# Moving each tile of a log-softmax as two transfers, its even and its odd partitions

## The chip, the cores and the metric

The kernel runs on one core of a Trainium2 chip. The core has five engines that take instructions of their own: PE (TensorE), DVE (VectorE), ACT (ScalarE), POOL (GpSimd) and SP (SyncE), and 16 DMA engines, which move data between the chip's main memory (HBM) and the core's on-chip buffer (SBUF, 128 partitions). The metric is the device time of one execution in microseconds (us). The kernel before takes 7580.06 us, the median of 8 runs between 7571.31 and 7588.07 us. The profile comes from one further execution, recorded by the hardware profiler, which took 7638.0 us.

## What is computed

A log-softmax along the last axis of a tensor of 16 x 512 x 50000 float32 numbers:

```python
def reference(x):
    max_x = np.max(x, axis=-1, keepdims=True)
    shifted = x - max_x
    log_sum_exp = np.log(np.sum(np.exp(shifted), axis=-1, keepdims=True))
    return (shifted - log_sum_exp).astype(np.float32)
```

The input and the output have 8192 rows of 50000 numbers each, 1638.40 MB read and as much written.

## The kernel before

**Tiles.** A tile is 32 rows. Each row is cut into four quarters of 12500 numbers, and a quarter is one partition: partition p holds quarter p mod 4 of row p div 4 (lines 73 and 74). So a tile fills 128 partitions with 12500 numbers (50000 bytes) each, 6.4 MB in all, and lies in main memory without a gap. There are 256 tiles and four buffers (`bufs`, line 93); tile t uses buffer t mod 4, and the result is written over the input in the same buffer.

**Loads.** SP issues them. The first tile comes as two transfers of half the columns each (lines 150 to 154), the next three as one transfer each (line 156). Then a loop (lines 158 to 161) waits for `stored[j]` to reach 16 (the helper `take`, line 47, which also takes the count back) and issues the load of the next tile into buffer j (line 148). A load adds 16 to `landed[j]` when it has landed, one for each DMA engine.

**Work on a tile.** DVE waits for `landed[j]` (line 201, by way of `take`), reduces four column blocks of 3125 numbers to their negated maxima (line 206), and joins these to one maximum for each row with a few small instructions (lines 171 to 186). ACT exponentiates each column block as its maximum is ready, with the sum accumulated beside it (line 248), and then makes four factors that bring the blocks' sums to the common maximum (line 256). DVE multiplies (line 217), PE adds up the four partitions of a row with a matrix of ones and zeros (line 285), ACT takes the logarithm (line 239), and DVE subtracts maximum and logarithm from the whole buffer in place (line 191).

**Stores.** ACT issues them (line 243): it waits until DVE has subtracted, issues one transfer for the buffer, and the transfer adds 16 to `stored[j]` when it is done. The last tile alone is subtracted and stored in four column blocks (lines 219, 278 and 279).

**Order.** There is no planner: each engine has its list of instructions, and semaphores tie the lists together. Loads go through the DMA queue of SP (q1 in the profile), stores through that of ACT (q10), each in the order of its engine's list. ACT has, for each tile, four exponentials, two small instructions and then the store; what is queued behind a store on ACT is the first exponential of the next tile.

Of the kernel before, what the change touches and what calls it, by code (L numbers as in the profile page):

```python
# [19 lines left out]
NBUF = 4  # L20

NS = 4

HEAD = 2

# [19 lines left out]
def take(engine, sem, n=16):  # L45

    engine.wait_ge(sem, n).then_inc(sem, -n)  # L47


def cols(c):  # L50
    return slice(c * C, (c + 1) * C)


@with_exitstack
def kernel(
# [9 lines left out]
    W = V // G  # L65
    assert N % R == 0 and W == NS * C
    ntiles = N // R
# [5 lines left out]
    xt = xf.rearrange("(t r) (g w) -> t (r g) w", r=R, g=G)  # L73
    ot = of.rearrange("(t r) (g w) -> t (r g) w", r=R, g=G)

    def run(a, first, n):

        part = a[first : first + NBUF * n].rearrange("(q i) p w -> q i p w", i=NBUF)
        return lambda q, i: part[bass.ds(q, 1), i].rearrange("o p w -> (o p) w")
# [13 lines left out]
    bufs = [data.tile([P, W], FP32, name=f"buf{j}") for j in range(NBUF)]  # L93
# [4 lines left out]
    def each(n, width, name):  # L98
        return [stats.tile([P, width], FP32, name=f"{name}{j}") for j in range(n)]

    negms, parts, scales, scaleds = (
        each(NBUF, NS, n) for n in ("negm", "part", "scale", "scaled")
    )
# [9 lines left out]
    def sem(name):  # L113
        return ctx.enter_context(nc.semaphore(name))

    landed = [sem(f"landed{j}") for j in range(NBUF)]
    stored = [sem(f"stored{j}") for j in range(NBUF)]
    heads = [sem(f"head{h}") for h in range(HEAD)]
    ready = sem("ones_ready")
    on_dve = Count(sem("on_dve"))  # L120
# [7 lines left out]
    subtracted = Count(sem("subtracted"))  # L128
# [3 lines left out]
    @block.gpsimd  # L132
    def _(gpsimd):
        view = ones.rearrange("p (r g) -> p r g", g=G)
        gpsimd.memset(ones, 1.0).then_inc(ready)  # L135
        gpsimd.affine_select(  # L136
            out=view, in_=view, pattern=[[-G, R], [0, G]], base=0,
            channel_multiplier=1, compare_op=ALU.is_ge, fill=0.0,
        ).wait_op(ready, 1, "sem-ge").then_inc(ready)
        gpsimd.affine_select(  # L140
            out=view, in_=view, pattern=[[G, R], [0, G]], base=G - 1,
            channel_multiplier=-1, compare_op=ALU.is_ge, fill=0.0,
        ).wait_op(ready, 2, "sem-ge").then_inc(ready)

    @block.sync
    def _(sync):
        def load(j, src):
            sync.dma_start(out=bufs[j], in_=src).then_inc(landed[j], 16)

        for h in range(HEAD):  # L150
            part = slice(h * W // HEAD, (h + 1) * W // HEAD)
            sync.dma_start(
                out=bufs[0][:, part], in_=xt[0][:, part]
            ).then_inc(heads[h], 16)
        for t in range(1, NBUF):
            load(t, xt[t])
        src = run(xt, NBUF, rounds)
        with sync.Fori(0, rounds) as q:
            for j in range(NBUF):
                take(sync, stored[j])  # L160
                load(j, src(q, j))
        for j in range(NBUF - 1):
            take(sync, stored[j])
        take(sync, stored[NBUF - 1], 16 * NS)

    @block.vector
    def _(vector):
        def share(k):

            on_dve.next(  # L170
                vector.transpose(out=allneg, in_=negp.to_broadcast([P, SQ]))  # L171
            ).then_inc(on_dve.sem)
            on_dve.next(
                vector.tensor_reduce(  # L174
                    out=rowneg, in_=allneg.rearrange("p (r g) -> p r g", g=G),
                    op=ALU.min, axis=AX,
                )
            ).then_inc(on_dve.sem)
            on_dve.next(
                vector.tensor_copy(  # L180
                    out=spread.rearrange("p (r g) -> p r g", g=G),
                    in_=rowneg[:, :, None].to_broadcast([P, SQ // G, G]),
                )
            ).then_inc(on_dve.sem)
            on_dve.next(
                vector.transpose(out=negmaxs[k], in_=spread)  # L186
            ).then_inc(agreed.sem)

        def subtract(k, *bufs):
            for n, buf in enumerate(bufs):  # L190
                ins = vector.tensor_scalar(  # L191
                    out=buf, in0=buf, scalar1=negmaxs[k][:, 0:1], scalar2=logs[k],
                    op0=ALU.add, op1=ALU.subtract,
                )
                if n == 0:
                    logged.next(ins)
                ins.then_inc(subtracted.sem)

        def whole(j, first=False, by_pieces=False):
            if not first:  # L200
                take(vector, landed[j])

            for c in range(NS):
                if first and c % (NS // HEAD) == 0:
                    take(vector, heads[c // (NS // HEAD)])
                vector.tensor_reduce(  # L206
                    out=negms[j][:, c : c + 1], in_=bufs[j][:, cols(c)],
                    op=ALU.max, axis=AX, negate=True,
                ).then_inc(shifted.sem if c < NS - 1 else on_dve.sem)
            on_dve.next(vector.nop()).then_inc(shifted.sem)  # L210
            vector.tensor_reduce(  # L211
                out=negp, in_=negms[j], op=ALU.min, axis=AX
            ).then_inc(on_dve.sem)
            share(j)

            rescaled.next(
                vector.tensor_mul(out=scaleds[j], in0=scales[j], in1=parts[j])  # L217
            ).then_inc(summed.sem)
            subtract(j, *([bufs[j][:, cols(c)] for c in range(NS)] if by_pieces else [bufs[j]]))

        def settle():
            for count in (on_dve, rescaled, logged):
                count.settle(vector)

        for j in range(NBUF):
            whole(j, first=j == 0)
        settle()
        with vector.Fori(0, rounds - 1):
            for j in range(NBUF):
                whole(j)  # L230
            settle()
        for j in range(NBUF):
            whole(j, by_pieces=j == NBUF - 1)

    @block.scalar
    def _(scalar):
        def log(k):
            added.next(
                scalar.activation(out=logs[k], in_=rowsums[k], func=ACT.Ln)  # L239
            ).then_inc(logged.sem)  # L240

        def store(j, dst, buf):
            subtracted.next(scalar.dma_start(out=dst, in_=buf)).then_inc(stored[j], 16)

        def whole(j):
            for c in range(NS):
                shifted.next(
                    scalar.activation(  # L248
                        out=dump, in_=bufs[j][:, cols(c)], func=ACT.Exp,
                        bias=negms[j][:, c : c + 1], scale=1.0,  # L250
                        accum_out=parts[j][:, c : c + 1],
                    )
                ).then_inc(on_act.sem)
                on_act.next(scalar.nop())  # L254
            agreed.next(
                scalar.activation(  # L256
                    out=scales[j], in_=negms[j], func=ACT.Exp,
                    bias=negmaxs[j][:, 0:1], scale=-1.0,
                )
            ).then_inc(rescaled.sem)  # L260
            log(j)

        def settle():
            for count in (on_act, shifted, agreed, added, subtracted):
                count.settle(scalar)

        nc.scalar.preload_act_table_set("natural_log_exp_and_others")  # L267
        dst = run(ot, 0, rounds)
        with scalar.Fori(0, rounds) as q:
            for j in range(NBUF):  # L270
                whole(j)
                store(j, dst(q, j), bufs[j])
            settle()
        for j in range(NBUF - 1):
            whole(j)
            store(j, ot[ntiles - NBUF + j], bufs[j])
        whole(NBUF - 1)
        for c in range(NS):
            store(NBUF - 1, ot[ntiles - 1][:, cols(c)], bufs[NBUF - 1][:, cols(c)])

    @block.tensor
    def _(tensor):
# [47 lines left out]
```

## Time and profile before

| What | Value |
|---|---|
| Median of 8 runs | 7580.06 us |
| The profiled execution | 7638.0 us, its span 7636.3 us |
| DVE busy | 5441.3 us (71% of the span) |
| ACT busy | 3184.7 us (42%) |
| PE busy | 477.9 us (6%) |
| Moved by DMA | 3276.85 MB, mean 429 GB/s |
| Median from issue to landing | load 44.4 us, store 48.5 us |

The span is the profiled execution from its first to its last instruction. An engine's busy time is the sum of its instructions; waiting is not counted. The page cuts the span into 40 equal slices, and in the row named DMA each digit is the busy share of the 16 DMA engines in a slice, in tenths, where 9 is 90% or more. A "packet" is one piece of a transfer that one DMA engine moves. "SPq" and "ACTq" are the instruction queues of SP and ACT, which wait and issue transfers; in a row such as "A <- B: 973.8, 253, 11.4", A waited for B for 973.8 us in total, 253 times, 11.4 us at the longest.

### The profile page before, as it was taken

What the parts mean: (1) busy time and instruction counts of PE and PEld (TensorE: products, weight loads), DVE (VectorE), ACT (ScalarE), POOL (GpSimd) and SP (SyncE); (2) the same over time, 40 slices, a digit from 0 to 9 for tenths busy, and PEclk for the clock granted to TensorE, in tenths of its full rate; (3) what the DMA queues carried; (4) which work ended last, traced back from release to release, by engine and by line L of the source; (5) the groups of instructions that cost most, each with busy time, mean ns of one, the idle gap of its engine ahead of it and who ended that gap; (6) DMA issues with size and microseconds to landing.
All of it is one profiled execution on the core that took longest, in us unless ns stands there. A gap on an engine that the chain in (4) does not pass through costs nothing. (4 is left out here: it accounts for less than half of the span.)

```text
span 7636.3 us, 14069 instructions
## 1 busy us (share of the span) xinstructions
PE 477.9 (6%) x2048; PEld 456.0 (6%) x2048; DVE 5441.3 (71%) x2819; ACT 3184.7 (42%) x2561; POOL 1.4 (0%) x7
## 2 busy tenths in 40 slices
PE   0000000000000000000000000000000000000000
PEld 0000000000000000000000000000000000000000
DVE  7777777777777777777777777777777777777766
ACT  4344444444344343434444344443434434444333
POOL 0000000000000000000000000000000000000000
DMA  9999999999999999999999999999999999999998
GB/s 427 432 435 433 435 433 435 433 435 433 434 432 432 433 432 435 432 434 433 434 433 429 431 427 430 429 428 431 432 427 431 428 428 430 427 426 427 427 414 368
DMA packets 74306, 3276.85 MB, mean 429 GB/s; under 512 B 8256, under 2 KB 8256, under 8 KB 8256
## 3 DMA queue, kind: packets, MB, share of 16 engines
q1 hardware_dynamic: 37008, 1638.42, 50.3%
q10 hardware_dynamic: 37296, 1638.42, 49.6%
q14 instruction: 2, 0.02, 0.0%
HBM read 1638.40 MB, written 1638.40 MB: 429 GB/s over the span
## 5 line engine op out<-in xcount | busy, mean ns | idle before, releaser
L248 ACT ACTIVATE dump<-buf,negm 128x3125 f32<-128x3125 f32 x1024 | 2937.2, 2868 | 3856.1 <-DVE negm L206 3758.6
L206 DVE TENSOR_REDUCE negm<-buf 128x1 f32<-128x3125 f32 x1024 | 3418.4, 3401 | 973.9 <-DVEq L47 973.8
L191 DVE TENSOR_SCALAR buf<-buf,negmax,logsum 128x12500 f32<-128x12500 f32 (+1 forms) x259 | 1739.0, 6715 | 553.8 <-ACT logsum L239 553.8
L285 PE MATMUL sums<-scaled,ones 128*128 128x1 f32 x2048 | 477.9, 355 | 7138.3 <-DVE scaled L217 7138.3
L285 PEld LDWEIGHTS sums<-scaled,ones 128*128 128x128 f32 x2048 | 456.0, 328 | 7160.1 <-DVE scaled L217 7160.1
L217 DVE TENSOR_TENSOR scaled<-scale,part 128x4 f32<-128x4 f32 x256 | 41.6, 163 | 580.2 <-ACT scale L256 580.2
L239 ACT ACTIVATE logsum<-sums 128x1 f32<-128x1 f32 x256 | 43.8, 171 | 551.1 <-PE sums L285 551.1
L248 ACT ACTIVATION_READ_ACCUMULATOR dump<-buf,negm 128x1 f32 x1024 | 190.8, 186 | 0.0
L256 ACT ACTIVATE scale<-negm,negmax 128x4 f32<-128x4 f32 x256 | 76.1, 297 | 23.6
L211 DVE TENSOR_REDUCE negp<-negm 128x1 f32<-128x4 f32 x256 | 40.2, 157 | 39.2 <-DVE negm L206 39.2
L186 DVE STREAM_TRANSPOSE negmax<-spread 128x32 f32<-128x32 f32 x256 | 54.2, 212 | 8.9
L171 DVE STREAM_TRANSPOSE allneg<-negp 128x32 f32<-128x32 f32 x256 | 54.2, 212 | 8.9
L174 DVE TENSOR_REDUCE rowneg<-allneg 128x8 f32<-128x32 f32 x256 | 47.7, 186 | 8.9
L180 DVE COPY spread<-rowneg 128x32 f32<-128x32 f32 x256 | 46.4, 181 | 8.9
L267 ACT ACT_TABLE_LOAD x1 | 1.3, 1283 | 1.0 <-SPq L111 1.0
L136 POOL TENSOR_SCALAR_AFFINE_SELECT ones<-ones 128x128 f32<-128x128 f32 x1 | 0.5, 519 | 0.1
L140 POOL TENSOR_SCALAR_AFFINE_SELECT ones<-ones 128x128 f32<-128x128 f32 x1 | 0.5, 519 | 0.1
L135 POOL MEMSET ones<- 128x128 f32 x1 | 0.2, 205 | 0.5 <-SPq L111 0.5
L314 POOL MEMSET const-bfloat16-1.0<- 128x1 bf16 x1 | 0.1, 103 | 0.0
L314 POOL MEMSET const-uint8-127<- 128x1 uint8 x1 | 0.1, 103 | 0.0
L314 POOL MEMSET const-float32-0.0<- 128x1 f32 x1 | 0.1, 99 | 0.3 <-issue 0.3
L314 POOL MEMSET const-float32-1.0<- 128x1 f32 x1 | 0.1, 99 | 0.0
## 6 DMA issues: line engine op xcount, KB each, us to landing
buf<-in_x_dram SPq DMA_DIRECT2D x255, 6250.0 KB, 44.4
out_dram<-buf ACTq DMA_DIRECT2D x255, 6250.0 KB, 48.5
buf<-in_x_dram SPq DMA_DIRECT2D x2, 3125.0 KB, 13.7
out_dram<-buf ACTq DMA_DIRECT2D x4, 1562.5 KB, 8.1
```

What stands on the lines that cost most here:

```text
L171: vector.transpose(out=allneg, in_=negp.to_broadcast([P, SQ]))
L174: vector.tensor_reduce(out=rowneg, in_=allneg.rearrange("p (r g) -> p r g", g=G), op=ALU.min, axis=AX,)
L180: vector.tensor_copy(out=spread.rearrange("p (r g) -> p r g", g=G), in_=rowneg[:, :, None].to_broadcast([P, SQ // G, G]),)
L186: vector.transpose(out=negmaxs[k], in_=spread)
L191: ins = vector.tensor_scalar(out=buf, in0=buf, scalar1=negmaxs[k][:, 0:1], scalar2=logs[k], op0=ALU.add, op1=ALU.subtract,)
L206: vector.tensor_reduce(out=negms[j][:, c : c + 1], in_=bufs[j][:, cols(c)], op=ALU.max, axis=AX, negate=True,).then_inc(shifted.sem if c < ...
L211: vector.tensor_reduce(out=negp, in_=negms[j], op=ALU.min, axis=AX).then_inc(on_dve.sem)
L217: vector.tensor_mul(out=scaleds[j], in0=scales[j], in1=parts[j])
L239: scalar.activation(out=logs[k], in_=rowsums[k], func=ACT.Ln)
L248: scalar.activation(out=dump, in_=bufs[j][:, cols(c)], func=ACT.Exp, bias=negms[j][:, c : c + 1], scale=1.0, accum_out=parts[j][:, c : c + 1],
L256: scalar.activation(out=scales[j], in_=negms[j], func=ACT.Exp, bias=negmaxs[j][:, 0:1], scale=-1.0,)
L285: ins = tensor.matmul(rowsums[j], ones, scaleds[j][:, c : c + 1], start=c == 0, stop=c == NS - 1,)
```

## The change

Each load and each store of a whole tile becomes two transfers: one of the 64 even partitions, one of the 64 odd ones. Each buffer has two semaphores for its stores, one for each half, and SP issues the load of a half as soon as the store of that half is done. DVE still waits for the whole tile: both loads add to the same `landed[j]`, and it now waits for 32. The first tile's load and the last tile's store stay as they were.

```diff
+H = 2
+def half(a, h):
+    return a.rearrange("(q h) w -> q h w", h=H)[:, h, :]
...
-    stored = [sem(f"stored{j}") for j in range(NBUF)]
+    stored = [[sem(f"stored{j}_{h}") for h in range(H)] for j in range(NBUF)]
...
-        def load(j, src):
-            sync.dma_start(out=bufs[j], in_=src).then_inc(landed[j], 16)
+        def load(j, src, h):
+            sync.dma_start(
+                out=half(bufs[j], h), in_=half(src, h)
+            ).then_inc(landed[j], 16)
...
         with sync.Fori(0, rounds) as q:
             for j in range(NBUF):
-                take(sync, stored[j])
-                load(j, src(q, j))
+                for h in range(H):
+                    take(sync, stored[j][h])
+                    load(j, src(q, j), h)
...
-                take(vector, landed[j])
+                take(vector, landed[j], 16 * H)
...
         def store(j, dst, buf):
-            subtracted.next(scalar.dma_start(out=dst, in_=buf)).then_inc(stored[j], 16)
+            for h in range(H):
+                ins = scalar.dma_start(out=half(dst, h), in_=half(buf, h))
+                if h == 0:
+                    subtracted.next(ins)
+                ins.then_inc(stored[j][h], 16)
```

More of the change, by code (lines that the diff above doesn't have):

```diff
@@ L155, in _ @@
         for t in range(1, NBUF):
-            load(t, xt[t])
+            for h in range(H):
+                load(t, xt[t], h)
         src = run(xt, NBUF, rounds)
@@ L159, in _ @@
             for j in range(NBUF):
-                take(sync, stored[j])
-                load(j, src(q, j))
+                for h in range(H):
+                    take(sync, stored[j][h])
+                    load(j, src(q, j), h)
         for j in range(NBUF - 1):
-            take(sync, stored[j])
-        take(sync, stored[NBUF - 1], 16 * NS)
+            for h in range(H):
+                take(sync, stored[j][h])
+        take(sync, stored[NBUF - 1][0], 16 * NS)
     @block.vector
@@ L242, in store @@
         def store(j, dst, buf):
-            subtracted.next(scalar.dma_start(out=dst, in_=buf)).then_inc(stored[j], 16)
+            for h in range(H):
+                ins = scalar.dma_start(out=half(dst, h), in_=half(buf, h))
+                if h == 0:
+                    subtracted.next(ins)
+                ins.then_inc(stored[j][h], 16)
         def whole(j):
@@ L278, in _ @@
         for c in range(NS):
-            store(NBUF - 1, ot[ntiles - 1][:, cols(c)], bufs[NBUF - 1][:, cols(c)])
+            subtracted.next(
+                scalar.dma_start(
+                    out=ot[ntiles - 1][:, cols(c)], in_=bufs[NBUF - 1][:, cols(c)]
+                )
+            ).then_inc(stored[NBUF - 1][0], 16)
     @block.tensor
```

## Prediction

> **What bounds the kernel now.** I read the page from the top: busy times, the 40 slices, then the DMA queues.
>
> ```profile
> span 7636.3 us, 14069 instructions
> PE 477.9 (6%) x2048; PEld 456.0 (6%) x2048; DVE 5441.3 (71%) x2819; ACT 3184.7 (42%) x2561; POOL 1.4 (0%) x7
> ...
> DMA  9999999999999999999999999999999999999998
> GB/s 427 432 435 433 435 433 435 433 435 433 434 432 432 433 432 435 432 434 433 434 433 429 431 427 430 429 428 431 432 427 431 428 428 430 427 426 427 427 414 368
> DMA packets 74306, 3276.85 MB, mean 429 GB/s; under 512 B 8256, under 2 KB 8256, under 8 KB 8256
> ...
> q1 hardware_dynamic: 37008, 1638.42, 50.3%
> q10 hardware_dynamic: 37296, 1638.42, 49.6%
> ```
>
> No compute engine is full, and the DMA engines are: the two queues' packets take 50.3% and 49.6% of the 16 engines' time, 99.9% together. The packet counts tell what a packet is. 257 loads on 16 engines make 4112 small packets, one for each engine to raise the semaphore, and 255 x 128 + 2 x 128 = 32896 data packets, one for each partition; the sum is 37008. The stores' 37296 come out likewise (255 x 128 + 4 x 128 + 259 x 16). So a partition's 50000 bytes are one packet. A load packet takes 0.503 x 16 x 7636.3 / 32896 = 1.87 us on average; the trace's packet records give a median of 1.847 us for both directions, and 9 ns for a small packet. 65536 packets' worth of data (50000 bytes each) on 16 engines at 1.847 us make 7565 us. That is 71 us less than the span, and only 15 us less than the median of the runs shown.
>
> Next, is a DMA engine ever without work? I asked for the DMA share by stretches; of each row the last two numbers are the share and the GB/s.
>
> ```profile
> 1000.00:2000.00 1000.00, 63.47 (x272) 60.55 (x272) 716.95 (x374) 422.79 (x340) 0.00 (x0) 1.00 1.00 434
> 5000.00:6000.00 1000.00, 63.49 (x272) 60.57 (x272) 710.14 (x368) 412.96 (x334) 0.00 (x0) 1.00 1.00 430
> 7000.00:7400.00 400.00, 26.14 (x112) 24.94 (x112) 277.75 (x148) 164.51 (x134) 0.00 (x0) 1.00 1.00 423
> 7500.00:7560.00 60.00, 3.74 (x16) 3.57 (x16) 40.90 (x22) 24.87 (x20) 0.00 (x0) 1.00 0.99 406
> 7560.00:7600.00 40.00, 1.86 (x8) 1.78 (x8) 25.58 (x13) 12.43 (x10) 0.00 (x0) 1.00 0.79 329
> 7600.00:7636.00 36.00, 1.87 (x8) 1.78 (x8) 19.11 (x14) 12.44 (x10) 0.00 (x0) 1.00 0.65 275
> ```
>
> The share is 1.00 up to about 7500 us. The slower late stretches are slower packets, mostly loads, not idle engines. Only the last 76 us have idle DMA time: 0.21 x 40 + 0.35 x 36 = 21 us.
>
> Last, the waits, DVE's and SP's, and the time of a transfer from issue to landing.
>
> ```profile
> DVE negm L206 <- DVEq L47: 973.8, 253, 11.4
> ```
> ```profile
> SPq L47 <- SPq L47: 7480.2, 256, 69.2
> ```
> ```profile
> buf<-in_x_dram SPq DMA_DIRECT2D x255, 6250.0 KB, 44.4
> out_dram<-buf ACTq DMA_DIRECT2D x255, 6250.0 KB, 48.5
> ```
>
> DVE waits 3.85 us per tile for the load. SP does nothing but wait for stores. But with about 29.6 us per tile (7565 / 256), 44.4 us means that 1.5 loads are under way on average, and 48.5 us that 1.6 stores are: each engine has something in line from at least one queue nearly always. The early refill shortens SP's wait, and thus adds to a line that is never empty.
>
> **The change part by part.** Against the profiled execution (span 7636.3 us, in all 7638.0):
>
> *Earlier refill of the first half.* The first half's store is half as long, so its load can be issued up to half of a store's flight (some 24 us) earlier, and stands in line that much longer. The second half goes out when the whole went before. In the steady stretch this is worth 0: what hides it is the full share of 1.00, and the same packets remain. DVE's 3.85 us go on being a wait for the DMA; what would be late next, if they went, is the DMA again. At the end it can help: what is loaded earlier leaves more stores for the 21 us that are idle now. So its worth lies between 0 and -21 us. I take 0, since the end hangs on one chain that doesn't change: last load, four maxima, sums, four subtractions (21.1 us from the first maximum at 7597.29 to the first store at 7618.41), four stores.
>
> *Twice as many transfers.* 255 more on each queue, 16 small packets each: 8160 x 9 ns / 16 = +4.6 us on every DMA engine. They stand among data packets on the path that sets the end, so all of it counts. Lower bound 0, if they overlap; upper bound +33 us, if each leaves a seam of 65 ns, the longest small packet in the records (8160 x 65 ns / 16). I take +4.6 us, since 9 ns is what nearly all of them take.
>
> *Issue time.* A store's issue on ACT takes 0.34 us (timeline, line 243), a second one adds as much per tile. Behind it on ACT waits the next tile's first exponential, which waits anyhow for the first maximum: ACT's waits for L206 come to 3758.6 us. Hidden, 0. Uncovered it would be 255 x 0.34 = 87 us. SP issues one more load and takes one more count per tile, and has 7480 us of waiting: 0. DVE's wait for 32 instead of 16 is one instruction as before: 0.
>
> *Which engine moves which partition.* This the trace doesn't show. Before, each transfer has 128 partitions, 8 for each engine; after, 64 with a step of two, 4 for each if all 16 still take part. Below, it could be a gain only if packets went faster than 1.847 us, and no steady row has that; so 0. Above, if two engines always met at the same part of SBUF and halved each other's speed, every packet would take 3.69 us: +7565 us. I take 0, as the 1.847 us is an even pace of each engine by itself, and the pieces keep their 50000 bytes.
>
> [...]
>
> *Sum.* 0 + 4.6 + 0 + 0: 7642.6 us for a profiled execution, 7584.7 us for the median of the runs, since the two stand 58 us apart before (slower packets in the profiled one) and nothing added depends on that.
>
> **The rivals.** A measurement of this kernel tells about 0.2% (15 us) from no change, so "the same" is 7565 to 7595 us.
>
> 1. *Nothing to tell, 7584.7 us: 0.44.* For it: share 1.00 and the smallness of everything added. Own range 7565 to 7595.
>
> 2. *Two DMA engines hinder each other, because 64 partitions with a step of two are dealt out otherwise than 128: 0.36.* The place is every data packet of a half; it decides as soon as the engines' mean packet time exceeds 1.847 us by 0.2%, since no slack is left. Price from part 3: were all load packets twice as long, +0.503 x 7636 = +3841 us (11,400); were it half of them, +1920 us, so 9500 us, my value for this case. Against it: a small overlap gives only per cents, as in the stretch at 423 GB/s (2.5% below 434).
>
> 3. *Small costs add up, or load packets slow down as in the late stretches: 0.10.* The seam of 65 ns makes 7580 + 33 = 7613 us, my value. A steady 430 instead of 434 GB/s (rows above) would make 7580 x 434 / 430 = 7651.
>
> 4. *Only half of the engines take part: 0.04.* Twice the DMA time, some 15,100 us. Against it: 64 divides by 16.
>
> 5. *The end gets shorter: 0.06.* All 21 us go and the small packets overlap: 7559 us. Against it: the last tile's chain, and the 15 us that are all the runs have above 7565.
>
> **The numbers.** Slower 0.36 + 0.10 + 0.04 = 0.50; same 0.44; faster 0.06. The likeliest single case is the first, so 7584.7 us is the prediction, though slower in all its forms is a little likelier. The range starts at 7559 us and has to reach far into case 2: of that I put six tenths below 9500 us, which leaves out 0.4 x 0.36 + 0.04 = 0.18.
>
> **What the profile after would show.** Right: DMA share 1.00 in the steady stretch, about 82,470 packets (74306 + 8160), GB/s at 427 to 435, load and store shares as before, DVE's wait for line 47 near 970 us. Case 2: still a share near 1.00, but fewer GB/s and longer packets in both queues, and DVE's waits up by what the span gains. Case 3: the share falls below 1.00, or only the loads' share rises. Case 4: a share near 0.5. Case 5: the last two slices above 414 and 368 GB/s. I am wrong if data packets no longer take 1.847 us, or if an end of 21 us turns out to be shortened by more than half.

## The result, and the profile after

The changed kernel takes 7616.16 us, the median of 14 runs (7596.31 to 7697.42), against 7581.6 us for the kernel before beside it (median of 40 runs, 7570.83 to 7593.02). The ratio is 1.0053 with a 95% interval of [1.004, 1.0065]: the medians are 35 us apart, more than the 0.2% that the prediction called no change. The ratio is higher than that of the medians since some runs are long: the means are 40 us apart. The ratios leave out runs more than 1.5% above the fastest of their kernel. Its profiled execution took 7627.38 us, less than the 7638.0 us of the profiled execution before. Which of the two profiles is the odd one is the first thing that the experiments had to settle.

From the page of the changed kernel, the span, the row of DMA shares and GB/s by slices, and the DMA queues:

```profile
span 7625.6 us, 15842 instructions
...
DMA  9999999999999999999999999999999999999999
GB/s 422 432 430 431 430 430 432 431 430 432 428 430 431 432 432 432 431 431 428 429 432 432 429 431 431 426 427 427 429 428 428 429 432 429 432 432 432 432 429 420
DMA packets 82466, 3276.88 MB, mean 430 GB/s; under 512 B 16416, under 2 KB 16416, under 8 KB 16416
...
q1 hardware_dynamic: 41088, 1638.43, 50.5%
q10 hardware_dynamic: 41376, 1638.43, 49.7%
```

The packets went up by 8160, all of them small, as counted. The DMA engines are as full as before. What differs is the height of the slices 2 to 21: mostly 430 to 432 GB/s where before had 432 to 435. The loads' share went from 50.3% to 50.5%, the stores' from 49.6% to 49.7%.

The last stretches of the span (share and GB/s are the last two numbers), and DVE's and SP's waits:

```profile
7500.00:7560.00 60.00, 3.73 (x16) 3.56 (x16) 42.86 (x23) 25.22 (x21) 0.00 (x0) 1.00 1.01 433
7560.00:7600.00 40.00, 1.86 (x8) 1.78 (x8) 31.27 (x19) 21.84 (x17) 0.00 (x0) 1.00 0.99 429
7600.00:7626.00 26.00, 1.86 (x8) 1.78 (x8) 7.52 (x5) 2.19 (x4) 0.00 (x0) 1.00 0.81 346
```
```profile
DVE negm L217 <- DVEq L49: 962.0, 254, 11.5
```
```profile
SPq L49 <- SPq L49: 7265.5, 511, 52.6
```

In this execution the end is fuller: 0.01 x 40 + 0.19 x 26 = 5 us of idle DMA time in place of 21. The section after the experiments shows whether the refill did that. DVE waits for loads as long as before (962.0 against 973.8 us), and SP still does little but wait (7265.5 of 7625.6 us).

### The profile page after: what moved, and what is told of

The parts are those of the page before. It is cut to its first block, busy times and chain, and to the rows that moved or that the text cites. A ratio compares the mean times of both kernels' runs of the same rounds, so it can differ in the third digit from the quotient of the medians.

```text
span 7625.6 us, 15842 instructions
## 1 busy us (share of the span) xinstructions
PE 477.9 (6%) x2048; PEld 455.9 (6%) x2048; DVE 5441.1 (71%) x2819; ACT 3184.6 (42%) x2561; POOL 1.4 (0%) x7
## 2 busy tenths in 40 slices
DMA packets 82466, 3276.88 MB, mean 430 GB/s; under 512 B 16416, under 2 KB 16416, under 8 KB 16416
## 3 DMA queue, kind: packets, MB, share of 16 engines
q1 hardware_dynamic: 41088, 1638.43, 50.5%
q10 hardware_dynamic: 41376, 1638.43, 49.7%
## 5 line engine op out<-in xcount | busy, mean ns | idle before, releaser
L217 DVE TENSOR_REDUCE negm<-buf 128x1 f32<-128x3125 f32 x1024 | 3418.4, 3401 | 962.0 <-DVEq L49 962.0
```

Source lines behind the costliest of these rows:

```text
L217: vector.tensor_reduce(out=negms[j][:, c : c + 1], in_=bufs[j][:, cols(c)], op=ALU.max, axis=AX, negate=True,).then_inc(shifted.sem if c < ...
```

## The experiments

All runs are compared with the kernel before on the same chip. A packet's duration is from the trace's packet records; 50000-byte packets if nothing else is said.

**Which profile is typical?** The kernel before, unchanged.

> The kernel before, unchanged, for a second profile and for the size of the noise. All theories: within 0.1% of the runs of before. Open is whether its profile again shows load packets of 1.847 us at first and longer ones, with one DMA engine some 25 us behind the others, in the later stretches (then 7638 us belongs to this kernel under the profiler), or not (then it was that one execution).

7587.4 us against 7585.44 us, ratio 1.0004 [0.9994, 1.0014]. Its profiled execution took 7586.85 us, and its slices stay near 433 GB/s to the end:

```profile
GB/s 426 434 432 433 433 434 434 433 433 432 431 433 431 432 432 434 434 432 434 434 435 434 433 433 435 432 434 432 433 434 434 434 432 434 434 433 433 432 433 397
```

So the late slow stretches in the first profile (428 GB/s and less) were that execution's. The prediction's profile was some 50 us slower than this kernel mostly is.

**Is it the early refill, the form of the loads, or the number of transfers?** Theory A: the load packets of a 64-partition transfer are slower by themselves. B: the early refill shifts loads against stores. C: each added transfer leaves a seam. First, refill only when both halves are stored:

```diff
                 for h in range(H):
                     take(sync, stored[j][h])
+                for h in range(H):
                     load(j, src(q, j), h)
```

> Both transfers halved as in the changed kernel (which is 0.53% slower, +40 us), but a half is refilled only when both halves have been stored. Theory A (the load packets of a 64-partition transfer are slower by themselves, whenever they are issued): +35 to +40 us, ratio 1.005, load packets of 1.87 us from the start. Theory B (the early refill is what costs: it shifts loads against stores): only the small packets are left, +5 us, ratio 1.0006. Theory C (each added transfer leaves a seam): +40 us, as the count is the same.

7623.77 us, +38 us, ratio 1.0047 [1.0033, 1.0061]: as the changed kernel (+35 us). **The early refill neither costs nor gains** anything that these runs can tell; B falls. The slices of this run:

```profile
GB/s 423 432 429 431 428 429 432 432 429 430 426 427 432 432 432 429 428 432 430 431 432 431 432 431 431 431 425 428 428 428 432 429 432 430 431 431 431 430 432 421
```

Then loads alone halved, stores whole, and the reverse:

```diff
             for j in range(NBUF):
+                take(sync, stored[j][0])
                 for h in range(H):
-                    take(sync, stored[j][h])
                     load(j, src(q, j), h)
...
-            for h in range(H):
-                ins = scalar.dma_start(out=half(dst, h), in_=half(buf, h))
...
+            subtracted.next(scalar.dma_start(out=dst, in_=buf)).then_inc(stored[j][0], 16)
```

> Loads halved, stores whole, both halves of the load issued when the whole store is done. Theory A: about all of the loss, +30 to +38 us. Theory B: +2 us. Theory C: half of the loss, +20 us.

7895.66 us, +310 us, ratio 1.0424 [1.0405, 1.0443].

```diff
-            sync.dma_start(
-                out=half(bufs[j], h), in_=half(src, h)
-            ).then_inc(landed[j], 16)
+            sync.dma_start(out=bufs[j], in_=src).then_inc(landed[j], 16)
...
                 for h in range(H):
                     take(sync, stored[j][h])
-                    load(j, src(q, j), h)
+                load(j, src(q, j))
```

> Stores halved, loads whole, issued when both halves are stored. Theory A: +2 to +5 us, as the loads are those of before. Theory B: +2 us. Theory C: +20 us.

7746.72 us, +161 us, ratio 1.0215 [1.0201, 1.0229].

No theory expected this: half of the change costs some five to nine times the whole (+35 us). The DMA queues of the run with loads alone halved, and a row of its stretches:

```profile
q1 hardware_dynamic: 41088, 1638.43, 51.0%
q10 hardware_dynamic: 37296, 1638.42, 48.8%
```
```profile
1000.00:2000.00 1000.00, 61.59 (x264) 58.76 (x264) 689.20 (x361) 405.18 (x328) 0.00 (x0) 1.00 1.00 415
```

The engines are full (99.8%), at 415 GB/s: the packets are longer on average. Loads average 1.958 us and stores 1.878 us, in place of 1.852 and 1.848 in the repeated run of before. Each engine moves 2040 of either, so 0.106 x 2040 + 0.030 x 2040 = 277 us of the 296 us between the two profiled executions (7882.4 and 7586.85).

**Do differently dealt partitions explain it?** Two new theories: P, engines hinder each other at SBUF where loads and stores deal partitions to engines differently; M, addresses under way together collide in main memory. Loads alone halved again, by columns, so that every transfer has all 128 partitions:

```diff
-    return a.rearrange("(q h) w -> q h w", h=H)[:, h, :]
+    return a[:, h * (a.shape[1] // H) : (h + 1) * (a.shape[1] // H)]
```

> As the run with loads alone halved (+310 us, ratio 1.0424), but a load's two halves are column halves of all 128 partitions, so each transfer keeps 8 partitions for each engine. Its load packets are 25000 bytes and twice as many. Theory P (engines hinder each other at SBUF where loads and stores deal their partitions to the engines differently): no hindering, only packets; a 25000-byte packet took 928 ns and a 50000-byte one 1847, so 9 ns x 2048 on each engine and the small packets, +21 us, ratio 1.003. Theory M (addresses of loads and stores under way together collide in main memory): no reason for it to be free, some per cent of loss as with even and odd halves. Theory C (added transfers leave seams): as the run with loads alone halved, 1.04.

7928.28 us, +341 us, ratio 1.0452 [1.0431, 1.0474]. Each transfer has the partitions of before and the loss stays, so P falls as the reason for it in this form; that even and odd halves lose for the same reason is not shown by it. M had expected some per cent here.

Lower and upper partitions in place of even and odd:

```diff
-    return a.rearrange("(q h) w -> q h w", h=H)[:, h, :]
+    return a[h * (P // H) : (h + 1) * (P // H), :]
```

> The changed kernel with lower and upper 64 partitions in place of even and odd ones; both halves, loads and stores, lie in one piece in main memory. Theory P, if 64 partitions are dealt out four in a row, with two engines at each part of SBUF: far slower, +25% to +100%, and in the first 60 us, where only loads run, half the pace of before, since one transfer of the changed kernel ran there at full pace. Theory M: within 1% of the changed kernel, either side. Theory C: as the changed kernel, +40 us.

10285.82 us, the median of 9806.57, 10216.19, 10355.45 and 10376.79 us, too far apart for an interval, against 7587.43 us: 29% to 37% slower. Two rows show it from the start, the changed kernel's and this one's; until 43 and 48 us only loads run:

```profile
30.00:60.00 30.00, 3.08 (x14) 2.91 (x14) 23.82 (x12) 12.61 (x11) 0.00 (x0) 1.00 1.02 418
```
```profile
30.00:60.00 30.00, 1.87 (x8) 1.78 (x8) 14.37 (x5) 4.42 (x7) 0.00 (x0) 1.00 0.94 248
```

By the landing records (mean over the 16 engines), the first halved load took 15.6 us after the transfer ahead of it with lower partitions, and 7.4 us with even ones (3125 KB in 7.4 us are 432 GB/s). The packets say the same: 3.92 us each there, 1.847 us in the changed kernel. So even partitions alone reach full pace, and 64 neighbouring ones half of it (3125 KB in 15.6 us are 205 GB/s). Here the halves also lie in one piece in main memory; that this is not the reason, the next run shows. Half the pace at the start is what P had expected here; its ground, that two engines meet at each part of SBUF, was my guess, and no run shows it.

**Is it the order in main memory?** Even and odd partitions in SBUF, but each half takes 64 neighbouring pieces of main memory:

```diff
+def piece(a, h):
+    return a[h * (P // H) : (h + 1) * (P // H), :]
...
-                out=half(bufs[j], h), in_=half(src, h)
+                out=half(bufs[j], h), in_=piece(src, h)
...
-                ins = scalar.dma_start(out=half(dst, h), in_=half(buf, h))
+                ins = scalar.dma_start(out=piece(dst, h), in_=half(buf, h))
```

> The changed kernel with the same even and odd partitions in SBUF, but each half takes 64 neighbouring pieces in main memory in place of every second one, for loads and stores alike. It leaves out that the quarters of a row come together: the sums are made over quarters of several rows, with the same instructions. Theory P: as the changed kernel, +40 us, load packets at 1.87 us. Theory M: the loss goes or changes by more than 15 us. Theory C: +40 us.

7606.65 us, +19 us, ratio 1.0034 [1.0012, 1.0056]: halves in one piece in main memory are not what cost 29% or more. Between the theories' numbers, so both were run once more, side by side:

> The changed kernel once more, beside the next one, to tell 35 us from 15 us on one chip. Theory M (every second piece in main memory lengthens load packets): +30 to +40 us, and 15 us or more above the next one. Rival: the two agree within 10 us, and the difference seen so far was that of the chips.

> Even and odd partitions in SBUF, neighbouring pieces in main memory, loads and stores, once more. It leaves out that the quarters of a row come together. Theory M: +5 to +20 us, load packets near 1.85 us. Rival: as the changed kernel.

The changed kernel: 7612.27 us, ratio 1.0037 [1.0019, 1.0055]; neighbouring pieces: 7610.87 us, 1.0028 [1.0016, 1.0041]. They don't differ by what these runs can tell; the rival is right, and M in the form tested here, the order of the pieces, has no support.

**Are there seams?** Four parts for each tile (`H = 4`).

> The changed kernel with four parts for each tile (every fourth partition, 32 in a transfer, 2 for each engine) in place of two. Theory C: three times the added transfers, so three times the loss, +120 us, ratio 1.016. Small packets alone: +14 us. Theory P: no fixed ratio; about that of the changed kernel plus 9 us, +50 us, if the deal puts the same engines at the same parts of SBUF, and per cents if it mixes them otherwise. Theory M: about as the changed kernel, as the same pieces are moved in nearly the same order.

7924.68 us against 7587.43 us, but its runs are too far apart for an interval: one took 7635.77 us (+48 us, about what P expected), the five others 7849.53 to 7965.42 us (+262 to +378 us). The profile is of one of these five:

```profile
GB/s 423 430 433 432 435 433 432 432 435 433 432 433 435 433 433 433 435 432 433 433 434 431 432 429 434 432 425 426 428 424 425 376 380 379 381 376 372 371 378 318
```
```profile
6300.00:7500.00 1200.00, 65.34 (x280) 62.35 (x280) 751.61 (x388) 439.25 (x353) 0.00 (x0) 1.00 0.94 377
```

For 26 slices (some 5000 us) it runs at the pace of before, with three times the added transfers; then it falls, in steps, to 376 and less. Seams would show in every slice: C falls. Why it falls later is open.

**Does it matter that loads and stores are cut alike?** Theory S: per cents are lost where they are cut differently. Theory N: halving loads costs per cents by itself. Both halved by columns (the edit of the column run, with the stores halved as well):

> Loads and stores both halved by columns, all 128 partitions in each, each half refilled when it is stored. Loads alone halved so cost +341 us. Theory S (loss of per cents comes where loads and stores are cut differently): only the doubled number of data packets is paid, 9 ns x 4096 = 37 us, and 5 us of small packets, +42 us, ratio 1.0055, packets at 928 ns in both queues. Theory N (smaller loads cost per cents by themselves): +340 us or more.

7620.12 us, +37 us, ratio 1.004 [1.0027, 1.0053]. With the stores cut like the loads, 341 us shrink to 37, and the slices hardly vary:

```profile
GB/s 425 432 432 432 432 432 433 432 432 432 432 432 432 432 432 432 432 432 432 432 432 432 432 432 432 432 432 432 432 432 432 431 432 429 430 429 432 431 431 375
```

A count covers the 37 us: packets of 929.4 and 928.9 ns on average in the two queues, fewer than 1% of them long, so 2 x 929 - 1848 = 10 ns on each of 4096 pairs, 41 us, and 5 us of small packets, somewhat more than was measured. N falls; S holds for halves, though not as a full account: four parts were cut alike, too, and lost 262 us and more in five of six runs. Last, loads alone halved, with neighbouring pieces of main memory:

> Loads alone halved, even and odd partitions in SBUF, but each half from 64 neighbouring pieces of main memory; stores whole. It leaves out that the quarters of a row come together. The same with every second piece cost +310 us. Theory M2 (the strided order in main memory is what costs there, too): below +100 us. Theory S (cut differently from the stores, whatever the order in memory): +200 to +400 us.

7885.15 us, +302 us, ratio 1.0396 [1.0381, 1.0411]: S again, and the order of the pieces in memory again without an effect to be seen. What makes unlike cuts slow is not shown.

## Where the changed kernel's 35 us are

The repeated run of the changed kernel shows it best; its slices, and two of its stretches:

```profile
GB/s 423 432 433 433 434 433 433 435 433 433 434 433 433 434 434 433 434 434 433 434 434 432 435 434 432 434 434 432 434 434 427 423 423 423 421 424 424 424 424 386
```
```profile
1000.00:4000.00 3000.00, 188.55 (x808) 179.89 (x808) 2150.98 (x1114) 1256.46 (x1011) 0.00 (x0) 1.00 1.00 434
6000.00:7000.00 1000.00, 63.46 (x272) 60.55 (x272) 701.59 (x364) 410.67 (x332) 0.00 (x0) 1.00 1.00 423
```

For three quarters of the span the changed kernel is as fast as the kernel before ever is (433 GB/s from 1000 to 4000 us in the repeated run of before). Then its load packets go from 1.847 to 1.94 us on average, the stores' stay at 1.848, and it runs at 421 to 424 until the last slice. It is not that every load packet is a little longer: from 6000 to 7000 us 36% of them take more than 1.87 us, 2.11 us on average, and the median stays at 1.847. In the kernel's first profile the load packets were at 1.876 us on average from 300 us on, 17% of them long. Time lost to long load packets is (mean - 1.847 us) x 2040 on each engine. The second thing that differs is the DMA engines' idle time in the last 100 us of the span, from the packet records:

| Profiled execution | us | mean load packet, us | lost, us | idle at the end, us | us without both |
|---|---|---|---|---|---|
| before, the first | 7638.0 | 1.8732 | 53 | 21 | 7564 |
| before, repeated | 7586.9 | 1.8524 | 11 | 15 | 7561 |
| changed, the first | 7627.4 | 1.8762 | 60 | 4 | 7563 |
| changed, repeated | 7627.1 | 1.8695 | 46 | 16 | 7565 |
| late refill | 7627.6 | 1.8765 | 60 | 3 | 7565 |
| neighbouring pieces | 7597.4 | 1.8536 | 13 | 20 | 7564 |
| neighbouring pieces, repeated | 7623.4 | 1.8679 | 43 | 16 | 7564 |

Without these two all seven are within 7561 to 7565 us, next to the 7565 us that 65536 packets of 1.847 us make. So in the profiles, the length of load packets and, less, the idle time at the end tell a fast execution from a slow one. Both kernels have such stretches, and in five executions of the halved forms four lost 43 us or more. The end's idle time doesn't follow the early refill: the late refill has 3 us, the changed kernel 4 and 16 us (last slices 421, 420 and 386 GB/s above).

For the runs without a profile, I infer the same: 5 us of the 35 are small packets (16416 of 9 ns each in two queues, against 8256), and the other 30 fit more or longer stretches of long load packets. That halving brings more of them is thus argued from the times, not shown: one of two profiles of before lost 53 us, too.

**What stays open** is why a stretch begins, and why halving by partitions would bring more of them. One DMA engine falling behind goes along with some: in the repeated run of the changed kernel the last of the 16 engines finished a transfer on average 3.5 us after the first at 300 to 600 us, 18 us at 5400 to 5700 us, and soon afterwards the stretch began; in the first profile of before the lag grew from 3.3 us (1500 us) to 19 us in loads and 23 us in stores (3900 us), where the load packets lengthened too. But the repeated run of before had a spread of some 20 us from 3900 us on with load packets of 1.85 us, and the first profile of the changed kernel had long packets with 3.4 us (300 to 1000 us). Nor do the runs say whether the engines hinder each other in SBUF, in memory or between; lower and upper halves show that the choice of partitions in SBUF can do it (10285.82 us, against 7606.65 us with even and odd ones and the same pieces of main memory), and the column run that packets also lengthen when each transfer has all the partitions (from 1000 to 2000 us 415 GB/s at a share of 1.00, against 432 with loads and stores both by columns).

## Why the prediction was right or wrong

- **Bound:** right. The DMA share stayed 1.00, and the losses found by the experiments are mostly longer packets, not idle engines. Two runs had some of both: four parts fell to a share of 0.94 at 377 GB/s, and in the run with loads alone halved by columns the two queues fill 98.9%.
- **Early refill, 0:** right; the late refill costs as much, +38 against +35 us. The prediction called itself wrong if the end's 21 us were shortened by more than half. In the changed kernel's first profile they were, to 5 us. But the late refill shows the same, and the changed kernel's repeated run has 16 us at the end, so the early refill is not what did it.
- **Twice as many transfers, +4.6 us:** right in price (9 ns each) and without the seams of the upper bound, which would have been +33 us: four parts add three times as many transfers and run for 26 slices at the pace of before.
- **Issue time, 0:** right, though the price was off: the two stores' issue took 1.29 to 1.44 us in the timeline, not twice 0.34. It stays hidden: the first exponential behind it starts 5.7 us after the issue, when the next maximum is ready (3711.97 and 3717.67 us).
- **Which engine moves which partition, 0 taken:** for even and odd halves alone the full pace of 432 GB/s bears it out, and the second rival (9500 us) fell for this choice. It was not an empty fear: with lower and upper halves it is +29% to +37%.
- **The failed step** of the likeliest case (7584.7 us, 31 us below the 7616.16 measured) is that "the same packets remain", with every packet kept at 1.847 us, and in the sum that "nothing added depends on" the slower packets of the profiled execution. The packets' size and number remained, not their duration: in the changed kernel's slow stretches 15 to 36% of the load packets are longer, which costs its two profiled executions 60 and 46 us. The prediction had seen such stretches (423 to 430 GB/s late in the span) and rightly put the 58 us between profile and median down to them, but gave the change no term for them. A second profile of before would have shown that they come and go.
- **What was luck.** The result is the third rival, load packets that slow down as in the late stretches, which had 0.10. Its value of 7613 us is near the measured time by luck: it came from a seam of 65 ns that the runs don't show. And the range was made wide for the second rival, which did not come.

## What to carry to other kernels

Compare packets x duration / 16 with the time first: here they agree within 0.2%, the DMA engines are full, and finer transfers and earlier refills gained nothing. If transfers have to be cut, try loads and stores cut alike, each spread over all partitions: here halves cut alike cost about 0.5%, unlike cuts 2 to 4.5%, and 64 neighbouring partitions 29 to 37%. Four parts cut alike cost 0.6% in one run and 3.5 to 5% in five, so alike is no guarantee. Before a per cent is argued from one profile, take it twice: two executions of the same kernel differed here by 51 us.

## What the runs showed of the hardware that I had not expected

- Halving loads alone cost +310 us, halving stores alone +161 us, both together +35 us.
- Four parts for each tile ran at 433 GB/s for some 5000 us and then broke down to 377 within one execution, with the program's loop unchanged.
- By the packet records 25000 bytes took 928 ns and 50000 bytes 1847 ns, so two packets of half the size take 9 ns more than one whole; a semaphore's packet took 9 ns.
- Long packets are a minority: halving loads alone raises the mean load packet to 1.958 us, but the median stays at 1.847 us, and 25% of them take more than 1.87 us.
